# Values of an attention layer stored whole and parted inside each head, with weight sums, constant rows and late loads placed anew, in an fp32 encoder trunk on Trainium2

## The chip, the cores and the metric

The kernel runs on one core of one Trainium2 chip. The metric is the device time of one execution in microseconds (us). A core has five engines that run side by side: PE (TensorE, matmul; PEld is its weight load), DVE (VectorE), ACT (ScalarE), POOL (GpSimd) and SP (SyncE), which here does nothing but issue DMAs. Each engine takes its instructions in order and waits on semaphores for the others; a DMA is issued from an engine's queue, in that queue's order, and lands later.

## The reference

A trunk of two layers over 1024 rows of width 1024, batch 1, all fp32. Layer 0 mixes with a gated MLP (mixer A), layer 1 with chunked attention against a shared K and V; each layer ends with a gated FFN (2816 wide, causal convolution of width 3).

```python
h = x
for l in range(DEPTH):                       # DEPTH = 2
    if l < N_A_LAYERS:                       # l == 0
        h = h + gmlp_mixer(rmsnorm(h, a_norm_g[l]), ...)
    else:                                    # l == 1
        kv = rmsnorm(h, kv_norm_g) @ w_kv
        k_shared, v_shared = jnp.split(kv, 2, axis=-1)   # (B, S, 16, 64) each
        h = h + chunk_attention(rmsnorm(h, b_norm_g[j]), k_shared, v_shared, b_w_q[j], b_rel_bias[j], b_w_o[j])
    h = h + conv_ffn(rmsnorm(h, f_norm_g[l]), f_w_in[l], f_conv_w[l], f_conv_b[l], f_w_down[l])
return rmsnorm(h, final_norm_g)
...
# chunk_attention, for a chunk of 64 queries and its band of 9 chunks of keys
sc = jnp.einsum('bqhd,bkhd->bhqk', qb, kb) + bias
p = jax.nn.softmax(jnp.where(valid, sc, NEG_INF), axis=-1)
o = jnp.einsum('bhqk,bkhd->bqhd', p, vb)
# conv_ffn
a = conv(h @ w_in) + conv_b
up, gate = jnp.split(a, 2, axis=-1)
return (jax.nn.silu(gate) * up) @ w_down
```

## The kernel before

**Products.** Every fp32 operand is parted into a high and a low part (`split`, L138 to L140: ACT casts the high part, `whi` or `yh`; DVE, sometimes POOL, subtracts it, giving `wlo` or `yl`), and a product is three matmuls, high × high, high × low and low × high. The large products are made by seven block products instead of eight (p = 1 to 7; the blocks are A11, A12, ..., and their sums are S1 to S4, made by `block_sum`, L383). A matmul is mostly 128x128 by 128x512.

**Order.** PE's instructions stand as the code is written. A counter, `tick`, adds up the duration of the matmuls issued so far; `put_off(us, fn)` calls `fn` once the counter has moved on by so much, and so places small pieces of work of other engines among the matmuls. Most other engines' instructions, and the DMAs on SP, are put in order by a scheduler that works with an estimated timeline; `issue_after` ties an instruction behind another one.

**Stages, with their places in the profile.** Mixer A to 295 us, FFN of layer 0 to 745. Then `down(0)`, 747 to 957: 77 steps, products 1, 6, 2, 7, 5, 4, 3 with 11 steps each, 12 matmuls a step (L992); each step needs one weight and one operand parted, which `make` does up to three steps ahead from loads of `load`; after the last step of a product `whole` adds the result into the residual h (POOL adds at L960 for products 6 and 7). Beside them the dictionary `aside` calls `value_sums(k)` at steps 46, 53, 60 and 67: load two rows of the value weights (`vr`), multiply both by the norm's gain on POOL (L1047), make four block sums on POOL (L383) and store them to DRAM (`vA`).

`norm` then scales h and parts it (`bc` and `dg` spread the row factors with a small matmul, L210), and makes four operand sums (`sums`). `values` (matmuls at L1141; weights parted into `vwh`, `vwl`) gives V by seven products; `out` parts each of the 8 × 2 result tiles and stores both parts in DRAM (`vd`: vhi and vlo, L1099). Among them q and k of the first pair of heads are made (L181 to L188).

**Heads.** Sixteen heads, 8 steps each, 1068 to 1465 us. A step makes scores (`st`, L1349 and L1351: `qe` by `km`, `qs` by `ks`), has DVE add the bias and ACT make the exponentials `p`, part them (`ph` on ACT, `pl` on POOL, L1363), and two steps later (LAG) multiplies by the value parts `vh`, `vl` (`po`, L1379 to L1383). The row maxima of the next head are made beside it: `mx` (L1196, L1202) and their transposed rows, `mr` (L1211, called by `mx.row`). `qe` and `km` hold some constant rows, copied by `constant_rows` out of tiles `e` (L1158, L1159); parity 0 and 1 of the heads have separate tiles QE, QS, KM, KS, VH, VL. Matmuls of later q and k (`fill`) are spread among the steps; START = 56 pieces of that fill stand before the first head. `stage` loads q and k of a head, `stage_v` its vh and vl. At the end of a pair `den` is inverted through DRAM (`few`, `rden`, `turned`) and the result stored as `osave` in two parts.

**Output projection and FFN of layer 1.** `load_o` loads the parts `oh`, `ol` of half t of the rows; the output projection runs 1465 to 1526 (`wo`), stores h, squares it (`sq`), and the FFN's first weights (`raw<-in_f_win`, cast to `whi`) follow from 1528 us.

## Time and profile before

| | |
|---|---|
| runs | 2181.34, 2181.42, 2186.42 us; median 2181.42 |
| profiled execution | 2186.06 us, of which the span is 2184.3 |
| mean granted TensorE clock | 0.986 |
| DVE, ACT, POOL busy | 74%, 49%, 37% of the span |
| HBM | 252 MB read, 118 MB written |

The profile page groups instructions as "line engine operation out<-in". An arrow with a name behind an idle time says what ended it. The clock is the share of full speed that TensorE was granted. PE's busy time counts matmuls as they are issued one behind the other, so a PE at half clock counts as busy. The stretches in the next section but one are cut at the stages above.

The page's 40 slices of 54.6 us show where PE (tenths busy) and its clock are below the rest:

```
PE   9999999999999999999699999899999999999998
PEclk9999999999999999999899999999999999999999
POOL 1084734333325116442355554431223332341020
DMA  7267623544537966934756766844234454578553
```

The dip is the twentieth slice, 1038 to 1092 us, the start of the heads.

### The profile page before, as it was taken

The numbers are of one execution on the slowest core, as the hardware profiler recorded it, in microseconds if no ns is written. First come the engines' busy times: TensorE is split into PE (matmuls) and PEld (weight loads), VectorE is DVE, ScalarE is ACT, GpSimd is POOL, SyncE is SP. The second block draws the span as 40 slices with busy tenths as digits, with TensorE's granted clock in tenths as the row PEclk, the third lists the DMA queues.
The fourth block names the chain that finished last, engine by engine and source line by source line (L and its number), as shares of the span: only waits on it lengthen the run. The fifth ranks groups of instructions, "written<-read, shape, count | busy, mean of one in ns | idle before, by whom it ended". The sixth has DMA issues, their size and how long they took to land.

```text
span 2184.3 us, 28950 instructions
## 1 busy us (share of the span) xinstructions
PE 2127.6 (97%) x9832; PEld 1770.1 (81%) x9832; DVE 1606.0 (74%) x2355; ACT 1076.2 (49%) x1879; POOL 798.5 (37%) x560
## 2 busy tenths in 40 slices
PE   9999999999999999999699999899999999999998
PEld 8888878888888887777588888787888888888887
DVE  5197889888888668886466655664888888885676
ACT  6423555444555543553366656552554455554443
POOL 1084734333325116442355554431223332341020
PEclk9999999999999999999899999999999999999999
DMA  7267623544537966934756766844234454578553
GB/s 251 75 211 258 240 81 102 169 154 158 171 135 252 341 230 206 315 128 145 212 127 165 178 145 157 228 128 144 83 131 154 153 168 143 184 259 319 193 191 136
DMA packets 224268, 394.09 MB, mean 180 GB/s; under 512 B 61148, under 2 KB 79964, under 8 KB 224120
## 3 DMA queue, kind: packets, MB, share of 16 engines
q1 hardware_dynamic: 221096, 386.79, 55.5%
q10 hardware_dynamic: 3024, 5.46, 0.7%
q8 instruction: 77, 1.26, 0.2%
q14 instruction: 71, 0.58, 0.1%
HBM read 251.99 MB, written 118.08 MB: 169 GB/s over the span
## 4 chain that ended last, share of the span: by engine, by line
PE 83%; DVE 9%; DMA 3%; issue 3%; ACT 1%; SPq 1%; POOL 0%; DVEq 0%; POOLq 0%; ACTq 0%
PE up L992 8%; PE gate L992 8%; PE up L370 7%; PE up L368 7%; PE up L373 7%; PE gate L373 5%; PE gate L368 5%; PE gate L370 5%; PE vps L503 4%; PE qkv L181 2%; PE qkv L188 2%; PE qkv L184 2%; DVE wlo L140 2%; PE v L1141 2%; DVE yl L140 2%
## 5 line engine op out<-in xcount | busy, mean ns | idle before, releaser
L140 DVE TENSOR_TENSOR wlo<-raw,whi 128x512 fp32r<-128x512 f32 x378 | 344.4, 917 | 150.3 <-ACT whi L139 149.9
L139 ACT CAST whi<-raw 128x512 fp32r<-128x512 f32 x378 | 233.3, 620 | 283.8 <-PE gate L992 204.6
L368 PE MATMUL up<-yh,whi 128*128 128x512 f32 x688 | 268.9, 391 | 2.7 <-ACT whi L139 2.0
L370 PE MATMUL up<-yh,wlo 128*128 128x512 f32 x688 | 269.0, 391 | 0.3 <-DVE wlo L140 0.3
L840 POOL TENSOR_TENSOR h<-a 128x512 f32<-128x512 f32 x44 | 83.0, 1887 | 405.5 <-DVE a L832 392.9
L1363 POOL TENSOR_TENSOR pl<-p,ph 128x640 fp32r<-128x640 f32 (+4 forms) x128 | 160.0, 1251 | 167.7 <-ACT ph L1362 125.6
L368 PE MATMUL gate<-th,whi 128*128 128x512 f32 x496 | 192.9, 389 | 0.0
L370 PE MATMUL gate<-th,wlo 128*128 128x512 f32 x496 | 192.9, 389 | 0.0
L373 PE MATMUL up<-yl,whi 128*128 128x512 f32 x688 | 184.3, 389 | 0.0
L140 DVE TENSOR_TENSOR yl<-raw,yh 128x512 fp32r<-128x512 f32 x172 | 153.3, 894 | 8.9 <-ACT yh L139 8.9
L368 PEld LDWEIGHTS up<-yh,whi 128*128 128x128 f32 x688 | 129.5, 188 | 31.1 <-ACT whi L139 2.4
L370 PEld LDWEIGHTS up<-yh,wlo 128*128 128x128 f32 x688 | 129.7, 188 | 27.5 <-DVE wlo L140 0.6
L373 PEld LDWEIGHTS up<-yl,whi 128*128 128x128 f32 x688 | 129.4, 188 | 27.4 <-POOL yl L140 0.5
L373 PE MATMUL gate<-tl,whi 128*128 128x512 f32 x496 | 132.8, 389 | 0.3 <-DVE tl L140 0.3
L139 ACT CAST whi<-S 128x512 fp32r<-128x512 f32 x160 | 99.1, 620 | 66.2 <-PE up L373 60.3
L140 DVE TENSOR_TENSOR wlo<-S,whi 128x512 fp32r<-128x512 f32 x160 | 130.2, 815 | 0.0
L992 PE MATMUL up<-yl,whi 128*128 128x512 f32 (+1 forms) x312 | 122.2, 392 | 4.7 <-DVE yl L140 4.6
L992 PE MATMUL up<-yh,whi 128*128 128x512 f32 (+1 forms) x312 | 121.0, 388 | 2.3 <-ACT yh L139 2.3
L992 PE MATMUL up<-yh,wlo 128*128 128x512 f32 (+1 forms) x312 | 121.1, 388 | 1.7 <-DVE wlo L140 1.7
L992 PE MATMUL gate<-yh,wlo 128*128 128x512 f32 (+1 forms) x312 | 120.7, 387 | 0.0
L992 PE MATMUL gate<-yh,whi 128*128 128x512 f32 (+1 forms) x312 | 120.5, 386 | 0.0
L992 PE MATMUL gate<-yl,whi 128*128 128x512 f32 (+1 forms) x312 | 120.4, 386 | 0.0
(399 smaller groups left out, 5428.9 us busy)
## 6 DMA issues: line engine op xcount, KB each, us to landing
raw<-in_f_win SPq DMA_DIRECT2D x88, 512.0 KB
gT<-h SPq DMA_DIRECT2D x88, 256.0 KB
h<-in_f_wdown SPq DMA_DIRECT2D x44, 512.0 KB
dS<-h SPq DMA_DIRECT2D x88, 256.0 KB
raw<-dS SPq DMA_DIRECT2D x40, 512.0 KB
raw<-gT SPq DMA_DIRECT2D x40, 512.0 KB
gB<-a SPq DMA_DIRECT2D x66, 256.0 KB
raw<-in_f_wdown SPq DMA_DIRECT2D x30, 512.0 KB
```

The costliest lines, as they stand in the source:

```text
L139: behind[S] = S.copy(hi, src)
L140: return eng.tensor_tensor(lo, src, f32(hi), op=ALU.subtract)
L181: nc.tensor.matmul(ps, wh[:, k, :], xs[k][0], start=k == first, stop=False)
L184: nc.tensor.matmul(ps, wl[:, k, :], xs[k][0], start=False, stop=False)
L188: nc.tensor.matmul(ps, wh[:, k, :], xs[k][1], start=False, stop=k == last)
L368: nc.tensor.matmul(ps, wh[:, k, :], xs[k][0], start=first and k == 0, stop=False, skip_group_check=True)
L370: nc.tensor.matmul(ps, wl[:, k, :], xs[k][0], start=False, stop=False, skip_group_check=True)
L373: nc.tensor.matmul(ps, wh[:, k, :], xs[k][1], start=False, stop=k == 3, skip_group_check=True)
L503: nc.tensor.matmul(ps, a, b, start=k == i == 0, stop=k == KD - 1 and i == 2)
L840: G.tensor_tensor(B[n], x, B.get(y) if isinstance(y, str) else y, op=ALU.subtract)
L992: nc.tensor.matmul(ps[:, cs], w[:, ms], x[:, cs], start=q == i == 0 and p in (1, 6, 5, 4), stop=q == NP - 1 and i == 2, skip_group_check=True)
L1363: marks[2] = G.tensor_tensor(pl[:, :n], pf[:, :n], f32(ph[:, :n]), op=ALU.subtract)
```

## The change

- **Value weight sums.** `value_sums(k)` becomes `value_load`, `value_gain` and `value_sum(k, n)`, called at separate steps of `down(0)`. The gain is an ACT multiplication instead of a POOL one; the sums are called one by one every second step.
- **Values.** `out` no longer parts a tile: it copies (ACT) or adds (DVE) into one tile and makes one store to one tensor `vd`. `stage_v` loads a head's values once, into the vl tile; later an ACT copy makes vh and POOL subtracts it from vl in place.
- **Constant rows** of parity 1 are loaded first, into four tiles instead of two in turn; then the `km` and `qe` rows of head 1, bias, the values, and the `qs` and `ks` rows. START is 64.
- **Late loads.** Three parts of half t = 1 are loaded four steps before the last head ends, into QS, VH and VL of the finished parity 0; the remaining five pairs have buffers of their own (six before, besides two in QS and KS). The FFN's first two weight blocks are tied behind the last o load, and its ring of four raw tiles is made of two pools.
- Smaller: the sums in `norm` come 4.5 us apart instead of 2.2; `turned` of the pairs whose result is stored is called after 10.5 instead of 9.0; `mx.row` after 1.2 instead of 0.5.

```diff
-START = 56
+START = 64
...
-                    put_off(7.5 + 2.2 * k, lambda k=k: sums(k))
+                    put_off(7.5 + 4.5 * k, lambda k=k: sums(k))
...
-            open_raw(4)
+            open_raw(3)
+            raws["q"], raws["n"] = raws["ctx"].enter_context(tc.tile_pool(name="wq", bufs=1, reuse_waits="tile")), 0
...
-                behind["load"] = nc.sync.dma_start(raw[i], f_win[l, i * NF + j])
+                with tc.issue_after(behind["o"].ins) if l and j < 2 else ExitStack():
+                    behind["load"] = nc.sync.dma_start(raw[i], f_win[l, i * NF + j])
...
-            with tc.issue_after(behind["adds"].ins):
-                G.tensor_tensor(rows[j], rows[j], cc[:, c:c + 1].broadcast_to([P, T]), op=ALU.mult)
...
+    def value_gain(k):
+        rows = held[k]
+        for j in range(2):
+            S.mul(rows[j], rows[j], col(C_KVG + k + 4 * j))
...
+    def value_sum(k, n):
+        nc.sync.dma_start(va[n][k], block_sum(held[k], n, lambda: vs.tile([P, H], F32, tag="vS", name="vS", bufs=8), G))
+
+    aside = {}
+    for k, (load, first) in enumerate(((24, 28), (28, 36), (38, 48), (48, 57))):
+        aside.setdefault(load, []).append(lambda k=k: value_load(k))
+        aside.setdefault(first - 1, []).append(lambda k=k: value_gain(k))
+        for i in range(4):
+            aside.setdefault(first + 2 * i, []).append(lambda k=k, i=i: value_sum(k, f"S{i + 1}"))
...
-        def out(n, t, m, src, eng=V):
-            hi, lo = (npl.tile([P, H], F32R, tag="acc", name=a, bufs=4) for a in ("vh", "vl"))
-            split(hi, lo, src, eng)
-            for d, a in zip(vd, (hi, lo)):
-                nc.sync.dma_start(d[4 * t + m, :, halves[n]], f32(a))
+        def out(n, t, m, ps, b=None):
+            c = npl.tile([P, H], F32, tag="acc", name="c", bufs=4)
+            if b is None:
+                S.copy(c, ps)
+            else:
+                V.tensor_tensor(c, ps, b, op=ALU.add)
+            nc.sync.dma_start(vd[4 * t + m, :, halves[n]], c)
...
-        def stage_v(hd):
-            for dst, a in zip((VH, VL), vd):
-                nc.sync.dma_start(f32(dst[hd % 2][:, :, rows[hd % 2][0]]),
-                                  a[:, :, hd * 64:(hd + 1) * 64].rearrange("b p c -> p b c"))
+        def stage_v(hd, wait):
+            vh, vl = (v[hd % 2][:, :, rows[hd % 2][0]] for v in (VH, VL))
+            nc.sync.dma_start(f32(vl), vd[:, :, hd * 64:(hd + 1) * 64].rearrange("b p c -> p b c"))
+            put_off(wait, lambda: split(vh, vl, f32(vl), G))
...
-        put_off(7.0, lambda: constant_rows(1, lambda: b2.tile([P, H], F32, tag="o", name="e")))
...
-                waits = (8.0, 8.0) if stays else (9.0, 9.0 if p < LAST - 1 else 6.5)
+                waits = (8.0, 8.0) if stays else (10.5, 9.0 if p < LAST - 1 else 6.5)
...
+        tags = cycle(("o", "o", "den", "den"))
+        constant_rows(1, lambda: b2.tile([P, H], F32, tag=next(tags), name="e"))
         for hs in halves:
-            stage(1, hs)
-        stage_v(0)
+            stage(1, hs, "me")
         bs, bm = {0: new_bias(0, 0)}, {1: new_bias(1, 1)}
+        stage_v(0, 8.0)
+        for hs in halves:
+            stage(1, hs, "s")
...
+            if s == NH * NB - 4:
+                for k, a in enumerate((QS[0], VH[0].rearrange("p n c -> p (n c)"), VL[0].rearrange("p n c -> p (n c)"))):
+                    load_o(k, 1, at=[a[:, hs] for hs in halves])
...
-                stage_v(hd + 1)
+                stage_v(hd + 1, 6.0)
...
-                    put_off(0.5, mx.row)
+                    put_off(1.2, mx.row)
...
-        for k in range(KD):
-            load_o(k, 1, wop, [(QS, KS)[k][0][:, hs] for hs in halves] if k < 2 else None)
+        for k in range(3, KD):
+            load_o(k, 1, wop)
```

Three places of the instruction order carry terms of the prediction. The first is POOL inside `down(0)`. Before, behind the h adds of product 7 (L960, on buffers h_85 and h_86) come the gains (L1047) and the sums (L383):

```order
L960 TENSOR_TENSOR h_86<-h_86,u 128x512
L1047 TENSOR_TENSOR vr<-vr,cc 128x1024 x4
L383 TENSOR_TENSOR vS<-vr 128x512
L383 TENSOR_TENSOR vS<-vS,vr 128x512
```

After (the same lines are L963 and L384), the h adds of product 6 are those on h_84, those of product 7 on h_85 and h_86:

```order
L384 TENSOR_TENSOR vS<-vr 128x512
L384 TENSOR_TENSOR vS<-vr,vS 128x512
L963 TENSOR_TENSOR h_84<-h_84,u 128x512 x4
L384 TENSOR_TENSOR vS<-vr 128x512
L384 TENSOR_TENSOR vS<-vS,vr 128x512
L384 TENSOR_TENSOR vS<-vr 128x512
L384 TENSOR_TENSOR vS<-vr,vS 128x512
L239 TENSOR_TENSOR acc<-acc,sq 128x512
L963 TENSOR_TENSOR h_85<-h_85,u 128x512
```

The gains are gone from POOL; twelve sums (the last two of them shown) stand ahead of product 6's adds, four between them and product 7's.

The second is SP at the start of the heads. Before, behind the last value stores (L1099) come the twelve q and k rows of head 1 (L1182), the values (L1314), bias, and e in two pairs (L1158):

```order
L1099 DMA vlo<-vl 128x512
L1182 DMA km_9468<-k0hi 64x512
L1182 DMA qe_9466<-q0hi 64x512
...
L1182 DMA ks_9469<-k0hi 64x512
L1314 DMA vh_9470<-vhi 128x8x64
L1314 DMA vl_9472<-vlo 128x8x64
L1218 DMA bias<-in_bias 128x256 x2
L1158 DMA e<-in_consts 64x512 x2
...
L156 DMA raw<-in_w_kv 128x1024
L1158 DMA e<-in_consts 64x512 x2
```

After (value store L1117, values L1326, e L1171, rows L1195, bias L1231):

```order
L157 DMA raw<-in_w_kv 128x1024
L1117 DMA vd<-c 128x512
L1326 DMA vl_9399<-vd 128x8x64
...
L157 DMA raw<-in_w_q 128x1024
L1171 DMA e<-in_consts 64x512 x4
L1195 DMA km_9395<-k0hi 64x512
L1195 DMA qe_9393<-q0hi 64x512
...
L1231 DMA bias<-in_bias 128x256 x2
L1195 DMA qs_9394<-q0hi 64x512
```

All four e stand in one piece ahead of the rows of head 1, and the load of the first head's values stands ahead of them.

The third is SP at the end of the heads and the start of layer 1's FFN. Before, the last osave stores (L1449, L1450) stand ahead of every o load of half 1 that has a buffer of its own (L1285, L1286), and the stores of h (L1587) ahead of the weights (L792):

```order
L1449 DMA osave<-oh 128x512
L1450 DMA osave<-ol 128x512
L1580 DMA h_14389<-hsave_89 128x512 x3
L1285 DMA oh<-osave 128x512
...
L1587 DMA hsave_90<-h_14390 128x512 x3
L1587 DMA hsave_90<-h_14389 128x512 x4
L1587 DMA hsave_90<-h_14391 128x512 x3
L792 DMA raw<-in_f_win 128x1024 x2
```

After (o loads L1298 and L1299, osave L1461, h stores L1606, weights L795):

```order
L1298 DMA vh_9397<-osave 128x512
L1228 DMA qe_9393<-mr 1x8x128
...
L1299 DMA vl_9399<-osave 128x512
L1299 DMA vh_9397<-osave 128x512
L1461 DMA osave<-oh 128x512
...
L1606 DMA hsave_90<-h_14339 128x512 x3
L795 DMA raw<-in_f_win 128x1024 x3
L1606 DMA hsave_90<-h_14338 128x512 x4
L1606 DMA hsave_90<-h_14340 128x512 x3
```

Loads into vh and vl (and qs) now stand ahead of the last osave stores, and three of the first four weight loads ahead of seven of the h stores.

More of the change, by code (lines that the diff above doesn't have):

```diff
@@ L97, in new_raw @@
     def new_raw(shape, name="raw"):
-        return raws["p"].tile(shape, F32, tag="raw", name=name)
+        raws["n"] = raws.get("n", 0) + 1
+        return raws["q" if "q" in raws and raws["n"] % 4 == 0 else "p"].tile(shape, F32, tag="raw", name=name)
     def open_places():
@@ L959, in whole @@
                     for x in ((h12,) if p == 6 else (h21, h22)):
-                        behind["adds"] = G.tensor_tensor(x, x, u, op=ALU.add)
+                        G.tensor_tensor(x, x, u, op=ALU.add)
                     return
@@ L980, in down @@
                 if n in aside:
-                    aside[n]()
+                    for fn in aside[n]:
+                        fn()
                 b = "a" if p in (1, 2, 5, 3) else "b"
@@ L1032, in trunk @@
     open_n(0)
-    vd = [dp.tile([NB, P, D], F32, name=f"v{n}") for n in ("hi", "lo")]
+    vd = dp.tile([NB, P, D], F32, name="vd")
     va = {f"S{i}": dp.tile([4, P, H], F32, name=f"vA{i}") for i in range(1, 5)}
@@ L1039, in value_rows, with value_load @@
         return w_kv[KD + n:KD + n + width, :, k, :].rearrange("m p c -> p m c")
-    def value_sums(k):
-        rows = [vs.tile([P, T], F32, tag="vr", name="vr") for _ in range(2)]
+    held = {}
+    def value_load(k):
+        held[k] = [vs.tile([P, T], F32, tag="vr", name="vr") for _ in range(2)]
         for j in range(2):
-            nc.sync.dma_start(rows[j].rearrange("p (m c) -> p m c", c=P), value_rows(0, k + 4 * j))
-            c = C_KVG + k + 4 * j
-            with tc.issue_after(behind["adds"].ins):
-                G.tensor_tensor(rows[j], rows[j], cc[:, c:c + 1].broadcast_to([P, T]), op=ALU.mult)
-        A = {f"A{n + 1}{j + 1}": rows[j][:, halves[n]] for n in range(2) for j in range(2)}
-        for n in va:
-            nc.sync.dma_start(va[n][k], block_sum(A, n, lambda: vs.tile([P, H], F32, tag="vS", name="vS", bufs=8), G))
+            nc.sync.dma_start(held[k][j].rearrange("p (m c) -> p m c", c=P), value_rows(0, k + 4 * j))
+    def value_gain(k):
+        rows = held[k]
+        for j in range(2):
+            S.mul(rows[j], rows[j], col(C_KVG + k + 4 * j))
+        held[k] = {f"A{n + 1}{j + 1}": rows[j][:, halves[n]] for n in range(2) for j in range(2)}
+    def value_sum(k, n):
[6 more added lines that the diff above has]
+            aside.setdefault(first + 2 * i, []).append(lambda k=k, i=i: value_sum(k, f"S{i + 1}"))
     with tc.tile_pool(name="vs", bufs=4, side="right", reuse_waits="tile") as vs:
-        down(0, gs, ds, hsave[0], lambda t, acc: norm(h, acc, t, X), {46 + 7 * k: lambda k=k: value_sums(k) for k in range(4)})
+        down(0, gs, ds, hsave[0], lambda t, acc: norm(h, acc, t, X), aside)
     close_psum()
@@ L1093, in tee @@
                 split(*b, h_all[TEES[RIGHT[p]]][:, :, m * P:(m + 1) * P], G if m % 2 else V)
-        def out(n, t, m, src, eng=V):
-            hi, lo = (npl.tile([P, H], F32R, tag="acc", name=a, bufs=4) for a in ("vh", "vl"))
-            split(hi, lo, src, eng)
-            for d, a in zip(vd, (hi, lo)):
-                nc.sync.dma_start(d[4 * t + m, :, halves[n]], f32(a))
-        def added(ps, b):
-            c = npl.tile([P, H], F32, tag="f", name="c")
-            V.tensor_tensor(c, ps, b, op=ALU.add)
-            return c
+        def out(n, t, m, ps, b=None):
[5 more added lines that the diff above has]
+            nc.sync.dma_start(vd[4 * t + m, :, halves[n]], c)
         def whole(p, m, ps):
@@ L1117, in whole @@
             elif p == 5:
-                out(1, 1, m, added(ps, s1[m]), G)
-                out(0, 1, m, added(ps, x[m]))
+                out(1, 1, m, ps, s1[m])
+                out(0, 1, m, ps, x[m])
             else:
-                out(1, 0, m, added(ps, s1[m]))
+                out(1, 0, m, ps, s1[m])
         todo = [(p, k) for p in order for k in range(4)]
@@ L1149, in trunk @@
     b0 = b0_ctx.enter_context(tc.tile_pool(name="b0", bufs=1, reuse_waits="tile"))
-    QE, QS, KM, KS = ([b0.tile([P, T], F32R, name=f"{n}0")] for n in ("qe", "qs", "km", "ks"))
+    KS, QE, QS, KM = ([b0.tile([P, T], F32R, name=f"{n}0")] for n in ("ks", "qe", "qs", "km"))
     mr0 = b0.tile([NB, P], F32R, name="mr0")
@@ L1282, in load_o @@
     def load_o(k, t, pool=None, at=None):
-        os_[t][k] = oh, ol = at or (tuple(pool.tile([P, H], F32R, tag=n, name=n, bufs=KD - 2) for n in ("oh", "ol")) if pool
+        os_[t][k] = oh, ol = at or (tuple(pool.tile([P, H], F32R, tag=n, name=n, bufs=KD - 3) for n in ("oh", "ol")) if pool
                                     else new_y())
@@ L1294, in trunk @@
             place.append(b1.tile([P, T], F32R, name=f"{n}1"))
-        VH, VL = ([b1.tile([P, NB, P], F32R, name=f"{n}{c}") for c in range(2)] for n in ("vh", "vl"))
-        put_off(7.0, lambda: constant_rows(1, lambda: b2.tile([P, H], F32, tag="o", name="e")))
+        VH, VL = ([(b1 if c else bt).tile([P, NB, P], F32R, name=f"{n}{c}", bufs=1) for c in range(2)] for n in ("vh", "vl"))
         for c in range(2):
```

## The prediction

> **What bounds the kernel now.** I read the page's first section, then busy time by stretches, then the list of PE's waits, then the order in time around the longest. Columns of the stretches: length; busy time (instructions) of PE, PEld, DVE, ACT, POOL; granted clock; DMA share; GB/s.
>
> ```profile
> PE 2127.6 (97%) x9832; PEld 1770.1 (81%) x9832; DVE 1606.0 (74%) x2355; ACT 1076.2 (49%) x1879; POOL 798.5 (37%) x560
> ...
> 747.00:850.00 103.00, 103.00 (x456) 85.26 (x456) 64.48 (x87) 47.07 (x84) 19.65 (x13) 1.00 0.71 247
> 850.00:960.00 110.00, 99.17 (x414) 76.85 (x413) 93.94 (x104) 54.75 (x100) 61.80 (x37) 0.96 0.71 233
> 960.00:1055.00 95.00, 91.18 (x393) 74.03 (x392) 74.67 (x115) 37.84 (x65) 33.54 (x22) 0.97 0.50 166
> ...
> 1070.00:1085.20 15.20, 0.09 (x2) 0.09 (x1) 0.43 (x1) 2.95 (x6) 3.88 (x6) 0.66 0.91 214
> 1085.20:1375.00 289.80, 285.32 (x1539) 249.50 (x1540) 181.46 (x499) 176.22 (x371) 152.07 (x133) 0.99 0.65 153
> 1250.00:1262.00 12.00, 10.03 (x48) 8.63 (x47) 5.58 (x19) 4.08 (x8) 7.31 (x6) 0.86 0.68 173
> 1375.00:1400.00 25.00, 19.12 (x81) 15.68 (x81) 13.27 (x33) 13.31 (x29) 7.33 (x7) 0.80 0.93 244
> 1465.00:1495.00 30.00, 27.27 (x100) 20.30 (x99) 13.12 (x23) 6.75 (x12) 2.59 (x3) 0.83 0.80 271
> 1495.00:1550.00 55.00, 52.66 (x227) 42.63 (x226) 30.19 (x46) 19.05 (x35) 12.85 (x10) 0.97 0.27 92
> ...
> 1980.00:2090.00 110.00, 110.00 (x487) 91.07 (x486) 67.26 (x92) 50.97 (x90) 18.66 (x13) 1.00 0.67 237
> ```
>
> PE is the bound: 97% of the span, and the change takes no matmul away. All that can be won is PE's idle time and the slower clock behind it. A stretch's loss is therefore its length less PE's busy time, plus (1 − clock) × length, good to half a hundredth of the clock. In the down projection of layer 1 (1980 to 2090) PE loses nothing and starts a matmul every 110/487 = 0.226 us; losses of several us each lie between 850 and 1550, where the change works. The waits behind them (total, times, longest):
>
> ```profile
> PE mx L1196 <- issue: 15.1, 1, 15.1
> PE up L992 <- DVE yl L140: 4.6, 9, 1.0
> PE mr L1211 <- ACT p L1359: 3.9, 1, 3.9
> PE wo L181 <- DMA oh<-osave: 2.7, 6, 0.6
> ...
> PE v L1141 <- DVE vwl L140: 2.4, 1, 2.4
> ...
> PE bc L210 <- ACT dg L209: 2.1, 1, 2.1
> PE up L368 <- ACT whi L139: 2.0, 1, 2.0
> ```
>
> What the clock term is, the order in time shows just after the 3.9 us wait: matmuls of 512 columns start 0.43 us apart, not 0.226.
>
> ```profile
> 1381.72 0.63 PE L184 MATMUL qkv<-yh,wlo 128*128 128x512 f32 x1
> 1382.15 0.63 PE L181 MATMUL qkv<-yh,whi 128*128 128x512 f32 x1
> ```
>
> **The change part by part.**
>
> *Value weight sums (850 to 960).* The loss is 10.8 idle + 0.04 × 110 = 4.4, so 15.2 us. POOL's h adds and gains in order of time say why, and groups by line: POOL's sums, an ACT cast (whole span), and one DVE line in 850 to 900 (13 of them) and, as the last row, in 2000 to 2100 (37), inside the second down projection, where no value sums run. After the bar stand the sum in us and the mean of one in ns.
>
> ```profile
> 837.16 13.22 POOL L960 TENSOR_TENSOR h<-h,u 128x512 f32<-128x512 f32 x8 [26.51 <-DVE u L958]
> 850.35 9.24 POOL L1047 TENSOR_TENSOR vr<-vr,cc 128x1024 f32<-128x1024 f32 x4
> ...
> L383 POOL TENSOR_TENSOR vS<-vr 128x512 f32<-128x512 f32 x8 | 13.3, 1660 | 0.1
> ...
> L139 ACT CAST whi<-raw 128x512 fp32r<-128x512 f32 x378 | 233.3, 620 | 283.8 <-PE gate L992 204.6
> ...
> L140 DVE TENSOR_TENSOR yl<-raw,yh 128x512 fp32r<-128x512 f32 x13 | 22.7, 1745 | 0.0
> ...
> L140 DVE TENSOR_TENSOR yl<-raw,yh 128x512 fp32r<-128x512 f32 x37 | 31.9, 862 | 1.0 <-ACT yh L139 1.0
> ```
>
> POOL runs h adds, gains and sums one behind the other. Each step of down has 12 matmuls (12 × 0.226 = 2.71 us) and needs two DVE splits; beside a busy POOL these take 2 × 1.75 = 3.49 us and don't fit, elsewhere 2 × 0.86 = 1.72 and do. The change takes 8 gains of 9.24/4 = 2.31 us, 18.5 us, off POOL and puts them on ACT, which has half of these 110 us free (54.75 busy); my estimate there is two casts of 128x512 (0.62 each) per gain, 10 us in all. The order shows 12 of the 16 sums (1.66 us each, 20 us) in one piece, ahead of product 6's h adds, and the last 4 ahead of product 7's. Such a piece can be borne: POOL was busy from 837.16 and PE still full at 850 (103.00 of 103), since operands are made up to three steps ahead and DVE spares 2.71 − 1.72 = 1 us a step elsewhere. The h adds alone are what the second down projection has, and it loses nothing. I take 13 of 15.2; bounds 0 (the sums collide where they now are) and 15.
>
> The Trainium skill (SBUF — State Buffer, "Who interferes with whom") states that a VectorE instruction with two SBUF inputs contends with a GpSimd instruction that reads SBUF, and that the loser blocks for the whole instruction. The 1.75 us against 0.86 agree. By it the moved sums block too: if all 16 ran without a break, 26.6 us, some ten steps would overrun by 3.49 − 2.71 = 0.78 us each, and this term would be 5 us, not 13; that is within the first rival.
>
> *Norm, values, first q/k (960 to 1055).* The loss is 3.8 + 0.03 × 95 = 2.9, so 6.7 us; the waits on dg (2.1) and vwl (2.4) belong to it: DVE is behind with the value weights' splits. The change splits the first of them among down's steps, spaces the sums of norm at 4.5 instead of 2.2, drops 16 subtractions that parted the outputs (DVE or POOL) and halves 32 stores. I take 4; bounds 0 and 6.5.
>
> *Constant rows (1055 to 1085).* SP's, ACT's and PE's rows:
>
> ```profile
> 1062.12 0.32 SPq L1099 DMA_DIRECT2D vlo<-vl  x1
> 1062.54 1.89 SPq L1182 DMA_DIRECT2D km<-k0hi  x1
> ...
> 1078.91 1.11 SPq L1158 DMA_DIRECT2D e<-in_consts  x2
> ...
> 1084.43 1.14 ACT L1159 CAST km<-e 64x512 fp32r<-64x512 f32 x2 [4.97 <-DMA e<-in_consts]
> ```
>
> SP is in order: the value stores drag to 1062, then 12 rows of k and q, then, among other loads, e in two pairs, since e had two buffers; the second pair, issued at 1078.91, lands 5.5 us later and its casts release mx near 1085. Now the four e go ahead of those rows, into four buffers, behind 16 stores fewer. Issued near 1062.5, with the same 5.5 us and 1.1 us of casts they are done near 1069. PE has run out of work at 1070 (0.09 us busy from there); the fill before the first head is now 8 matmuls longer (8 × 0.226 = 1.8 us) and ends near 1072. So the 15.1 us mostly go; what is late next is the last q and k rows and the vl of the first head, and I leave 1 us for them. I take 14; bounds 8 (the copy of the first vl holds SP for some 6 us) and 17 (with 0.01 × 290 = 2.9 of clock in the next stretch, most of it not of this wait).
>
> *Each head.* One load of 256 KB instead of two; added are one ACT copy vh (512 values a lane, bounded by 0.62) and one POOL subtraction. Nearest rows:
>
> ```profile
> L1363 POOL TENSOR_TENSOR pl<-p,ph 128x512 fp32r<-128x512 f32 x12 | 16.0, 1330 | 21.0 <-ACT ph L1362 21.0
> ...
> 1252.17 1.90 POOL L159 TENSOR_TENSOR raw<-raw,cc 128x1024 f32<-128x1024 f32 x1 [5.05 <-PE st L1349]
> ```
>
> In 1085 to 1375 POOL is busy 52%, ACT 61%, PE 98%; 12 heads × 1.33 = 16 us more make POOL 58%. No throughput limit is near. The danger is order: POOL and ACT stand in line, and if the load is late the p work behind it waits. Such an event is there already: POOL's gain at 1252 sat in front of pl, PE waited 2.0, and the stretch 1250 to 1262 lost 2.0 + 0.14 × 12 = 3.7 us. The subtraction is called 6.0 us after the load's issue, e took 5.5 to land. Later mx.row (0.5 to 1.2) gives the row more time. I take 0; bounds −8 (two such events) and +4 (none is left).
>
> *1375 to 1400.* Loss 5.9 + 0.20 × 25 = 5.0, so 10.9.
>
> ```profile
> 1373.82 0.44 SPq L1457 DMA_DIRECT2D few<-den  x1
> ...
> 1378.47 0.20 DVE L1431 RECIPROCAL few<-few 128x8 f32<-128x8 f32 x1 [2.69 <-DMA few<-den]
> ```
>
> few landed 4.7 us after its issue, behind o loads, and the reciprocal stopped DVE for 2.69, then mr. The reciprocal is now called 1.5 us later and mx.row 0.7 later. 1.5 of 2.7 covers half: I take 5; bounds 0 and 9.
>
> *The last o-parts (1465 to 1495).* Loss 2.7 + 0.17 × 30 = 5.1, so 7.8.
>
> ```profile
> 1464.55 0.32 SPq L1449 DMA_DIRECT2D osave<-oh  x1
> ...
> 1474.23 0.32 SPq L1286 DMA_DIRECT2D ol<-osave  x1
> ...
> 1475.56 0.32 SPq L1286 DMA_DIRECT2D ol<-osave  x1
> ```
>
> SP waits until 1464.55 for the last heads' oh, then issues six pairs of o loads until 1475.56, the last 1.3 us behind the one before; PE waits for six of them. Three parts are now loaded ahead of the blocked store, so five pairs stand behind it: the last is 1.3 us earlier and the first ones no longer matter. I take 2; bounds 0 and 6.
>
> *Start of layer 1 (1495 to 1550).* Loss 2.3 + 0.03 × 55 = 1.7, so 4.0.
>
> ```profile
> 1521.80 4.67 SPq L792 DMA_DIRECT2D raw<-in_f_win  x2
> ...
> 1527.47 1.12 ACT L139 CAST whi<-raw 128x512 fp32r<-128x512 f32 x2
> ```
>
> The weights' casts stood behind sq of the last block. The loads now go behind the last o load, ahead of the stores. I take 3.5; bounds 0 and 4.
>
> Sum: 13 + 4 + 14 + 0 + 5 + 2 + 3.5 = 41.5. The profiled execution took 2186.06 (span 2184.3); that gives 2144.6. The median of the three runs is 2181.42, the others 2181.34 and 2186.42, so the profile is of the slower kind by 4.6; from the median it is 2139.9. I predict 2140.
>
> The Trainium skill (TensorE: Matmul & The Clock Gate, "What's actually happening") states that the array falls to half clock after an idle window of about 3.4 us. The clock of 0.83 in 1465 to 1495, where no wait is over 0.6, does not fit that rule alone. By it the clock parts of the last two terms would not hang on these waits, and the sum would be about 2 us smaller.
>
> **The rivals.**
>
> *The sums still collide.* The vr rows and the vA stores now share SP with down's loads earlier. If a store waits on POOL in front of a load, 850 to 960's loss only moves: 13 back, 2153. For: POOL still has 26.6 us of sums. Against: they stand in pieces of 20 and 7 us, not of 60.
>
> *The constant rows stay late.* Ahead of e on SP stand a raw load and the vl of head 0, which waits for POOL's memset, which waits for a gain whose load is late. If SP is held there some 10 us, 10 of the 14 stay: 2150. That is also how this part would fail to do what it says. For: POOL stood 6.58 us for that load (row below). Against: its gain ended at 1059.5, ahead of the 1062.5 reckoned with.
>
> ```profile
> 1057.62 1.90 POOL L159 TENSOR_TENSOR raw<-raw,cc 128x1024 f32<-128x1024 f32 x1 [6.58 <-DMA raw<-in_w_kv]
> ```
>
> *Slower: the copy waits in every head.* vh<-vl stands on ACT between the exponentials of p. If the load lands after the copy's turn, PE waits as at 1252, 3.7 us with the clock. Fifteen heads are 56 us: 2196. It decides from 41.5/3.7 = 11 heads on; with ten or eleven the time stands still, near 2180. For: 6.0 against 5.5 is a thin margin, and DMA share is 0.65. Against: half as much is loaded, and value matmuls stand two blocks behind the scores.
>
> **How the numbers follow.** Forecast 0.54; sums collide 0.18; rows late 0.14; heads stalling in ten or eleven 0.07, in all 0.07. A change of 0.3%, 6.5 us, is about what a measurement of this kernel can tell from none. The first three are faster by more: 0.86. Ten or eleven heads is the same: 0.07; all is slower: 0.07. The upper bounds of the terms lie 20 us above the values taken; two thirds of that, 14 us, gives the lower end, 2126. The upper end, 2168, is both rivals of the first kind at once, 13 + 10, and 5 for the small terms; the heads' cases, 0.14, lie outside.
>
> **What would show it.** Right: PE full from 850 to 940; mx's wait under 3 us, and km casts before 1072 on the old scale; DVE's reciprocal waiting under 1; no wait on whi at the start of layer 1. Wrong: up L992 still waiting on yl; the e loads behind a long gap of SP; PE waiting for po or mr in most heads with ACT idle in front of vh. If the stretches from 850 to 1550 gain less than 25 us in all, the forecast is wrong whatever the time.

## The result and the profile after

| | before | changed |
|---|---|---|
| median of four runs, us | 2182.20 (2181.34 to 2186.42) | 2153.56 (2148.97 to 2155.22) |
| ratio, 95% interval | | 0.9862 [0.9841, 0.9883] |
| profiled execution, us (span) | 2186.06 (2184.3) | 2148.97 (2147.2) |
| granted TensorE clock | 0.986 | 0.996 |

The change makes the kernel 28.6 us (1.4%) faster; 41.5 was forecast. The two profiles are 37.1 us apart, because that of before is near its slowest run and that of the changed kernel is its fastest. The difference between 28.6 and 37.1 is therefore not to be explained by an edit.

PE's order of matmuls is the same up to the last one of V, so up to there a stage can be cut at the same matmul in both traces. The next two fences show busy time by stretches, first the changed kernel, then the kernel before, with the columns of the prediction. The cuts are: first matmul of the second product of `down(0)`; first of V; last of V; start of head 1; of head 13; of head 15; first `wo` on `oh`; first matmul of layer 1's FFN. (The first product of `down(0)` takes 717 to 747 us in the kernel before and its last matmul is at 943; the 747 to 957 given for the whole of it above is not right. The cut at `wo` lies 0.45 us later in the changed kernel than at the same matmul, since its third part is in `vl` and not in `oh`.)

```profile
747.35:933.72 186.37, 183.58 (x804) 150.98 (x803) 135.96 (x175) 99.05 (x171) 57.91 (x37) 0.99 0.76 261
933.72:1042.50 108.78, 103.06 (x457) 83.65 (x456) 75.43 (x120) 43.29 (x76) 32.66 (x22) 1.00 0.47 151
1042.50:1079.00 36.50, 36.33 (x182) 30.77 (x181) 15.63 (x41) 19.89 (x39) 21.77 (x21) 1.00 0.63 154
1079.00:1355.60 276.60, 270.21 (x1464) 233.31 (x1462) 179.18 (x476) 175.70 (x370) 160.45 (x140) 1.00 0.60 154
1355.60:1404.50 48.90, 42.20 (x219) 35.49 (x219) 36.51 (x87) 31.05 (x65) 24.45 (x20) 0.97 0.71 192
1404.50:1445.80 41.30, 40.01 (x197) 33.92 (x198) 25.65 (x43) 18.94 (x36) 11.52 (x9) 1.00 0.36 118
1445.80:1492.80 47.00, 44.64 (x197) 35.87 (x196) 24.39 (x37) 12.32 (x22) 7.68 (x6) 1.00 0.53 191
```

```profile
747.04:943.10 196.06, 187.33 (x803) 150.40 (x802) 149.08 (x175) 90.59 (x163) 77.16 (x45) 0.98 0.72 245
943.10:1055.00 111.90, 105.98 (x458) 85.74 (x457) 84.01 (x130) 49.03 (x86) 37.82 (x26) 0.97 0.50 167
1055.00:1106.60 51.60, 36.49 (x175) 30.78 (x174) 18.93 (x44) 20.59 (x39) 19.42 (x19) 0.87 0.60 157
1106.60:1388.60 282.00, 273.66 (x1470) 238.69 (x1469) 174.56 (x476) 169.23 (x357) 145.51 (x129) 0.98 0.70 165
1388.60:1434.00 45.40, 41.85 (x219) 35.54 (x218) 34.81 (x88) 30.52 (x63) 21.34 (x19) 0.96 0.78 212
1434.00:1473.60 39.60, 39.43 (x196) 33.41 (x194) 24.17 (x43) 18.55 (x36) 12.17 (x10) 1.00 0.31 104
1473.60:1528.10 54.50, 49.95 (x198) 39.08 (x198) 22.84 (x36) 11.50 (x21) 8.15 (x6) 0.91 0.42 145
```

Row by row the changed kernel is shorter by 9.7, 3.1, 15.1, 5.4, −3.5, −1.7 and 7.5 us. The first three and the last are what the change aims at. In the heads (rows four and five) 327.4 became 325.5; the fill that now stands ahead of the first head, 8 matmuls or 1.8 us, is as much as that, so nothing was won there. PE's list of waits in the changed kernel names what stands there now:

```profile
PE st L1361 <- DMA qe<-mr: 7.2, 6, 3.2
PE wo L182 <- DMA oh<-osave: 2.3, 3, 1.1
PE mr L1224 <- DVE h L1219: 2.0, 1, 2.0
PE v L1154 <- DVE vwl L141: 2.0, 3, 0.7
PE po L1391 <- DVE o L1420: 1.9, 2, 1.3
...
PE up L996 <- DVE wlo L141: 1.6, 1, 1.6
...
PE up L996 <- DVE yl L141: 1.2, 1, 1.2
```

The wait of 15.1 us for `mx` is gone, and so are those on `whi` at the FFN's start and of `mr` for 3.9. The largest is now `st` waiting for the row of maxima (`qe<-mr`), 7.2 us in six waits after 0.7 in two; the two waits of `up` stand near 787 us, where there were none.

### The profile page after: what moved, and what is told of

Its sections match the earlier page's. It is cut to its first block, busy times and chain, and to the rows that moved or that the text cites. A ratio compares the mean times of both kernels' runs of the same rounds, so it can differ in the third digit from the quotient of the medians.

```text
span 2147.2 us, 28888 instructions
## 1 busy us (share of the span) xinstructions
PE 2110.6 (98%) x9832; PEld 1758.6 (82%) x9832; DVE 1586.6 (74%) x2343; ACT 1085.2 (51%) x1891; POOL 795.3 (37%) x564
## 4 chain that ended last, share of the span: by engine, by line
PE 80%; DVE 9%; DMA 5%; issue 2%; ACT 2%; POOL 1%; SPq 0%; DVEq 0%; POOLq 0%; ACTq 0%
PE up L996 8%; PE gate L996 8%; PE up L369 7%; PE up L371 7%; PE up L374 7%; PE gate L369 5%; PE gate L374 5%; PE gate L371 5%; PE vps L504 4%; PE qkv L182 2%; PE v L1154 2%; PE qkv L185 2%; DVE wlo L141 2%; PE qkv L189 2%; PE ups L182 1%
## 5 line engine op out<-in xcount | busy, mean ns | idle before, releaser
L369 PE MATMUL gate<-th,whi 128*128 128x512 f32 x496 | 192.9, 389 | 0.0
L371 PE MATMUL gate<-th,wlo 128*128 128x512 f32 x496 | 192.9, 389 | 0.0
L141 DVE TENSOR_TENSOR yl<-raw,yh 128x512 fp32r<-128x512 f32 x172 | 146.8, 856 | 10.0 <-ACT yh L140 9.2
L140 ACT CAST yh<-raw 128x512 fp32r<-128x512 f32 x190 | 115.1, 617 | 11.4 <-DMA raw<-gB 6.4
```

The costliest lines, as they stand in the source:

```text
L140: behind[S] = S.copy(hi, src)
L141: return eng.tensor_tensor(lo, src, f32(hi), op=ALU.subtract)
L369: nc.tensor.matmul(ps, wh[:, k, :], xs[k][0], start=first and k == 0, stop=False, skip_group_check=True)
L371: nc.tensor.matmul(ps, wl[:, k, :], xs[k][0], start=False, stop=False, skip_group_check=True)
```

## The experiments

All twelve were timed in five rounds. The changed kernel's median, 2153.6, is the measure for those that start from it. They ran in three groups (e1 to e4, e5 to e8, e9 to e12), each on another chip; the kernel before, timed beside each group, took 2181.9, 2181.7 and 2181.0, so medians of different groups compare to about 1 us. Medians with their ranges, and two stages of each profile between the cuts named above (changed kernel: 186.4 and 325.5 us):

| run | what is different | median us (range) | `down(0)` to V | head 1 to head 15 |
|---|---|---|---|---|
| e1 | mx.row after 0.5 | 2153.8 (2147.5 to 2155.5) | 187.5 | 328.9 |
| e2 | constant rows late, in two tiles | 2162.1 (2153.2 to 2170.2) | 184.9 | 324.8 |
| e3 | value sums as before | 2164.3 (2159.3 to 2175.5) | 198.2 | 327.6 |
| e4 | values parted before they are stored | 2159.3 (2155.9 to 2168.7) | 185.8 | 331.4 |
| e5 | reciprocal after 9.0 | 2144.5 (2141.4 to 2146.1) | 187.2 | 320.4 |
| e6 | reciprocal after 13.5 | 2179.0 (2171.1 to 2183.0) | 185.5 | 346.3 |
| e7 | sums behind product 6's adds | 2154.6 (2148.8 to 2156.3) | 186.9 | 328.8 |
| e8 | o-parts loaded as before | 2154.2 (2152.2 to 2156.9) | 185.0 | 330.0 |
| e9 | reciprocal 9.0 and mx.row 0.5 | 2143.3 (2139.5 to 2147.6) | 185.3 | 324.5 |
| e10 | reciprocal 9.0, sums in three pieces | 2150.9 (2143.4 to 2154.0) | 192.9 | 321.1 |
| e11 | kernel before, reciprocal 10.5 | 2180.5 (2173.1 to 2190.9) | 195.6 | 324.9 |
| e12 | weight loads not tied | 2153.0 (2149.5 to 2158.9) | 187.4 | 329.9 |

### e1: the row of maxima as early as before

```diff
-                    put_off(1.2, mx.row)
+                    put_off(0.5, mx.row)
```

> The changed kernel with mx.row called 0.5 us after step 5 again, not 1.2. Theory A (the row of maxima, moved back 0.7 us, now lands in qe after the next head's first score wants it): PE's waits of st on qe<-mr fall from 7.2 us in six to under 2, the time to about 2148 (2145 to 2151). Rival B (mr was waiting for its operands, so the wait only changes its place): mr waits 3 to 6 us in total for DVE or ACT, time 2152 to 2156.

The time did not move, 2153.8. `st` on `qe<-mr` waited 8.6 us, no less than the 7.2 of the changed kernel, and `mr` waited 4.4 us for DVE's maxima, as rival B said. Theory A falls: the moment at which the row is called is not what makes it late. The trace of the changed kernel says what does. SP's queue, in order of time, ahead of head 7:

```profile
1210.37 0.37 SPq L1445 DMA_DIRECT2D rden<-few  x1
1211.57 0.24 SPq L1417 DMA_DIRECT2D den<-den  x1
1212.83 1.41 SPq L1447 DMA_DIRECT2D den<-rden  x2
1214.35 0.69 SPq L1228 DMA_DIRECT2D qe<-mr  x1
```

and PE's rows there:

```profile
1210.33 0.27 PE L1224 MATMUL mr<-ident,mb 128*8 128x128 f32 x1
1216.63 0.35 PE L1361 MATMUL st<-qe,km 128*128 128x256 f32 x1 [1.33 <-DMA qe<-mr]
```

The row's matmul is at 1210.33, its store is issued 4.0 us later. In between SP stands at `den<-rden`, which reads what `rden<-few` has stored and waits until that has landed (18.7 us in 13 such waits in the heads, by SP's list). Where nothing delays it, as in heads 8, 10 and 12, the store follows the matmul by 0.63 us, and `st` starts 4.6 to 4.8 us behind it without a wait.

### e2: the constant rows late again

```diff
-        tags = cycle(("o", "o", "den", "den"))
-        constant_rows(1, lambda: b2.tile([P, H], F32, tag=next(tags), name="e"))
+        put_off(7.0, lambda: constant_rows(1, lambda: b2.tile([P, H], F32, tag="o", name="e")))
         for hs in halves:
-            stage(1, hs, "me")
-        bs, bm = {0: new_bias(0, 0)}, {1: new_bias(1, 1)}
+            stage(1, hs)
         stage_v(0, 8.0)
-        for hs in halves:
-            stage(1, hs, "s")
+        bs, bm = {0: new_bias(0, 0)}, {1: new_bias(1, 1)}
```

> The changed kernel with the constant rows of parity 1 loaded behind the rows of head 1 again, in two tiles by turns. Theory A (their place in SP's order was the whole stall): one wait of mx near 1070 us of 12 to 15 us, time 2166 to 2170. Rival B (half as many value stores free SP early enough by themselves): a wait of 4 to 8 us, time 2157 to 2162.

8.5 us slower in the median, at the far edge of rival B's range. The profile caught the fastest of the seven runs, with this wait:

```profile
PE mx L1209 <- issue: 4.4, 1, 4.4
```

From the end of V to head 1 that run took 43.5 us, against 36.5. The place in SP's order was thus about half of the 15.1 us that the stage had gained (7.0 by this profile, 8.5 by the medians), not all of it. The runs spread over 17 us, more than in any other kernel that starts from the changed one; a stall that hangs on when DMAs land would do that, but it was not shown.

### e3: the value sums as before

```diff
-    for k, (load, first) in enumerate(((24, 28), (28, 36), (38, 48), (48, 57))):
...
+            with tc.issue_after(behind["adds"].ins):
+                G.tensor_tensor(rows[j], rows[j], cc[:, c:c + 1].broadcast_to([P, T]), op=ALU.mult)
...
+    ... {46 + 7 * k: [lambda k=k: value_sums(k)] for k in range(4)}
```

> The changed kernel with the value weight sums as before: steps 46, 53, 60 and 67, gains on POOL. Theory A (a busy POOL stretches DVE's splits until operands are late): PE loses 11 to 13 us between 855 and 900 again, none near 787, time 2161 to 2166. Rival B (this stretch depended on what SP carried, which is less now): a loss of 5 or less, time 2152 to 2157.

10.7 us slower, and `down(0)` takes 198.2 instead of 186.4. PE's waits for it:

```profile
PE up L996 <- DVE yl L141: 6.8, 9, 1.7
PE up L996 <- DVE wlo L141: 2.4, 3, 1.3
```

They stand at 861 to 889 and 940 to 943 us, none near 787. Theory A holds. In the rows one by one, a split of DVE takes 0.68 us where POOL rests and 1.77 beside POOL's sums in the changed kernel, and 2.38 beside the gains (2.34 each) in the kernel before.

### e4: the values parted again before they are stored

```diff
+        def out(n, t, m, src, eng=V):
+            hi, lo = (npl.tile([P, H], F32R, tag="acc", name=a, bufs=4) for a in ("vh", "vl"))
+            split(hi, lo, src, eng)
+            for d, a in zip(vd, (hi, lo)):
+                nc.sync.dma_start(d[4 * t + m, :, halves[n]], f32(a))
...
+            for dst, a in zip((VH, VL), vd):
+                nc.sync.dma_start(f32(dst[hd % 2][:, :, rows[hd % 2][0]]),
+                                  a[:, :, hd * 64:(hd + 1) * 64].rearrange("b p c -> p b c"))
```

> The changed kernel with the values parted and both parts stored at values, and both loaded in each head. Theory A (the parting inside the heads costs nothing, the stores it saves are worth 2 to 5 us at the start of the heads): time 2155 to 2159, a wait near 1056 us of 2 to 5. Rival B (ACT's copy and POOL's subtraction delay p in the heads by 3 to 8 us in all): time 2146 to 2151, PE's waits in the heads that much smaller.

5.7 us slower, just above theory A's range; but the wait that it expected at the start of the heads is small (1.35 us at 1061.73), and the stage from V to head 1 takes only 2.0 us longer. V takes 2.8 us longer (111.6 against 108.8), and the heads, with twice the value loads, 5.9; of this last figure little can be put down to the edit, since e8 and e12, which leave the values alone, take 4.5 and 4.4 longer there.

### e5: the reciprocal after 9.0 us again

```diff
-                waits = (8.0, 8.0) if stays else (10.5, 9.0 if p < LAST - 1 else 6.5)
+                waits = (8.0, 8.0) if stays else (9.0, 9.0 if p < LAST - 1 else 6.5)
```

> The changed kernel with the reciprocal of den called after 9.0 us again, not 10.5. Theory A (called later, its chain few, rden, den through DRAM stands on SP in front of qe<-mr and makes st of the next head late): in heads 3, 7, 11 and 13 SP issues qe<-mr within 2.5 us of the row's matmul, not after 3 to 4; waits of st on qe<-mr fall from 7 to under 4 us, time 2148 to 2152. Rival B (the order on SP is the same, so the store stays late): waits of 7 or more, time 2152 to 2157, and DVE waits for few again.

9.1 us faster than the changed kernel: 2144.5, below theory A's range. The ranges of the two don't touch, though the intervals of their ratios to before overlap by a little (0.9834 [0.9817, 0.9850] and 0.9862 [0.9841, 0.9883]). SP ahead of head 7 in this run, where the row's matmul is at 1210.76:

```profile
1208.10 0.36 SPq L1445 DMA_DIRECT2D rden<-few  x1
...
1209.84 1.11 SPq L1447 DMA_DIRECT2D den<-rden  x2
1211.04 0.54 SPq L1462 DMA_DIRECT2D osave<-ol  x1
1212.28 0.24 SPq L1417 DMA_DIRECT2D den<-den  x1
1213.13 0.70 SPq L1228 DMA_DIRECT2D qe<-mr  x1
```

`rden` is stored 2.7 us ahead of the row's matmul and not with it, its landing is over in time, and `qe<-mr` goes out 2.4 us after the matmul instead of 4.0. In heads 3, 7 and 11 this is 1.6, 2.4 and 2.1 us (3.2, 4.0 and 3.2 in the changed kernel), and `st` waits there 0.3 us in all, not 2.0. DVE's own rows show why 1.5 us were enough. Changed kernel, then e5:

```profile
1210.16 0.19 DVE L1443 RECIPROCAL few<-few 128x8 f32<-128x8 f32 x1
```

```profile
1207.88 0.19 DVE L1443 RECIPROCAL few<-few 128x8 f32<-128x8 f32 x1
```

Called 1.5 us later the reciprocal falls back behind six instructions in DVE's order: relative to the row's matmul it stands at −0.2 and at −2.9 us. Head 13 waits longer than before the edit (3.45 us, SP again at `den<-rden`), so the sum of the waits on `qe<-mr`, 5.5 us, is above what theory A expected. The two waits of `po` for DVE's copy into `o`, 1.9 us, are gone as well.

The longest wait of the changed kernel, 3.25 us ahead of head 14, has another cause. There `qe<-mr` is issued 1.6 us behind the matmul in both kernels, but `st` starts 5.7 us after the issue in the changed kernel and 3.6 in e5: the transfer itself is slow. Two o loads (`yh<-osave`, `yl<-osave`) went out from 2.2 us ahead of it and not from 4.1, and the DMA share until `st` was 1.00 and not 0.75; that they slow it is likely, but not shown. The nine profiles with 10.5 take 5.2 to 6.0 us here, the four with 9.0 take 3.0 to 3.8. So the later reciprocal costs in two ways, and the waits ahead of heads 3, 7, 11 and 13, where SP stands at `den<-rden`, are 2.5 of the 7.2 us.

### e6: the reciprocal later still

`waits` begins with 13.5, else as above.

> The changed kernel with the reciprocal of den called after 13.5 us, so that the second den<-rden of a pair stands behind qe<-mr on SP. Theory A: qe<-mr is issued within 2 us in heads 3, 7 and 11, no wait of st on it there; PE's waits on qe<-mr fall from 7 to about 4 (head 14 stays), time 2147 to 2151. Rival B (the late part is the landing, not the issue, or o's two buffers now block): st still waits 6 or more, or po on DVE o waits over 4, time 2153 to 2160.

What each theory said of the waits came true, and the time lies outside both ranges. `qe<-mr` is issued 0.6 us after the matmul in heads 3, 7 and 11, its wait is down to 1.0 us, and the kernel is 25 us slower. PE's list:

```profile
PE po L1391 <- DVE o L1420: 24.8, 6, 7.1
PE po L1391 <- ACT vh L140: 3.1, 1, 3.1
```

`o` has two buffers; the later the division, the later one comes free for the copy out of PSUM, and the next head's `po` stands. Rival B, with a larger price than expected.

### e7 and e10: other places for the sums

e7 ties all 16 sums behind product 6's adds; e10 (on e5) ties them in pieces of 4, 8 and 4, ahead of, between and behind the two groups of adds. The tie of e7, and that of e10:

```diff
+        with tc.issue_after(behind["adds"].ins):
+            tile = block_sum(held[k], n, lambda: vs.tile([P, H], F32, tag="vS", name="vS", bufs=8), G)
+        nc.sync.dma_start(va[n][k], tile)
```

```diff
+        with tc.issue_after(behind["adds7" if k == 3 else "adds6"].ins) if k else ExitStack():
```

> The changed kernel with the value sums tied behind product 6's h adds on POOL (16 in one piece between the adds of products 6 and 7). Theory A (near 787 us the sums on POOL and their vA stores on SP delay product 6's adds and down's loads): no wait near 787; the stretch from the start of down to the first value matmul is 4 to 5 us shorter, time 2147 to 2151. Rival B (16 in one piece, 27 us, outlast DVE's lead): the loss of 4 to 8 us only moves to 800 to 830, time 2152 to 2158.

> The changed kernel with the reciprocal after 9.0 us and the 16 value sums on POOL in three pieces: 4 ahead of product 6's h adds, 8 between the adds of products 6 and 7, 4 behind product 7's. Theory A (a piece of 8 sums, 13 us, is borne by DVE's lead, one of 12 or 16 isn't): the stretch from the start of down to the first value matmul is 185 us or less, against 187.2, time 2140 to 2143. Rival B (the waits come from SP, whose vA stores wait for POOL between down's loads, however the sums are cut): 186 to 189 us, time 2143 to 2148.

e7: no wait near 787, but three of `up` on `yl` (0.85, 0.66 and 1.18 us) at 806, 815 and 820; `down(0)` 186.9, the time unchanged. Rival B, at the lower end. e10 is 6.3 us slower than e5, and outside both expectations: the waits near 787 stay (0.71 and 1.18 us) though no sum runs in the 21 us ahead of product 6's adds, and a new one of 2.91 us appears at 884.3, where ACT had stood 6.05 us for the value weights' loads (`raw<-in_w_kv`), issued 10.5 us later than in e5, with down's casts behind it. The size of a piece is not the cause near 787. In the changed kernel the twelve sums did not even run in one piece: POOL takes four from 752, four from 760 and four from 777 us, each time as soon as ACT has made the gains. What the waits near 787 begin with is ACT and DVE, here in the changed kernel:

```profile
774.41 1.15 ACT L1055 ACTIVATE vr<-vr,cc 128x1024 f32<-128x1024 f32 x1 [1.24 <-DMA vr<-in_w_kv]
775.91 1.15 ACT L1055 ACTIVATE vr<-vr,cc 128x1024 f32<-128x1024 f32 x1 [0.35 <-DMA vr<-in_w_kv]
777.25 0.62 ACT L140 CAST whi<-raw 128x512 fp32r<-128x512 f32 x1 [0.19 <-DMA raw<-in_f_wdown]
777.90 1.07 DVE L141 TENSOR_TENSOR wlo<-raw,whi 128x512 fp32r<-128x512 f32 x1 [3.92 <-ACT whi L140]
```

```profile
784.37 0.69 DVE L961 TENSOR_TENSOR u<-up,s 128x512 f32<-128x512 f32 x1 [1.24 <-POOL h L963]
785.63 0.69 DVE L961 TENSOR_TENSOR u<-gate,s 128x512 f32<-128x512 f32 x1 [0.56 <-POOL h L963]
786.24 1.13 DVE L141 TENSOR_TENSOR wlo<-raw,whi 128x512 fp32r<-128x512 f32 x1
```

The gains wait on ACT for their loads, with down's cast behind them; DVE gets the cast 3.92 us late and then waits 1.80 us with `u` (two buffers) for POOL's adds, with the split that PE needs behind it. The traces separate the two. In e7 DVE waits for the adds nearly as long (1.30 us) and PE waits for nothing near 787; but no `vr` is loaded between 748 and 790, ACT waits for no load from 760 to 792, and DVE's longest wait for a cast in the 10 us ahead of the adds is this:

```profile
774.34 0.69 DVE L141 TENSOR_TENSOR wlo<-raw,whi 128x512 fp32r<-128x512 f32 x1 [1.42 <-ACT whi L140]
```

In e10 it is 5.54 us, in the changed kernel 3.92. So DVE's lead had been spent on late casts, behind gains and loads that the change had moved there. This is read from the traces; no run moved the loads and gains alone.

### e8 and e12: the late loads

e8 puts all eight o-parts of half 1 behind the last osave store again, with VH and VL of parity 0 in their old pool; e12 takes the tie off the weight loads.

```diff
-                with tc.issue_after(behind["o"].ins) if l and j < 2 else ExitStack():
-                    behind["load"] = nc.sync.dma_start(raw[i], f_win[l, i * NF + j])
+                behind["load"] = nc.sync.dma_start(raw[i], f_win[l, i * NF + j])
```

> The changed kernel with the o-parts of half 1 loaded as before: all eight behind the last osave store, VH and VL of parity 0 in their old pool. Theory A (the early three parts shorten the chain by one pair and start it ahead): the stretch from the first wo on oh to the FFN's first matmul is 3 to 5 us longer, waits on oh 6 times again, time 2156 to 2159. Rival B (the part that went was the start of the FFN, by the earlier weight loads): 0 to 2 us longer, time 2153 to 2155.

> The changed kernel without the tie that puts the FFN's first weight loads of layer 1 behind the last o load (its ring of raw tiles stays in two pools). Theory A (the tie is what starts the casts in time): a wait of up on whi near 1493 us of 1.5 to 2.5 us again, the stretch from the first wo on oh to the FFN 3 to 5 us longer, time 2156 to 2159. Rival B (the scheduler puts the loads early by itself): no such wait, time 2151 to 2156.

Neither moves the time (2154.2 and 2153.0), and neither brings the wait on `whi` back. e12's order shows why: without the tie the first three weight loads go even earlier on SP, ahead of the first h store. The stretch from the first `wo` on `oh` to the FFN was 47.1 us in the changed kernel, 52.0 in e8 and 52.1 in e12, but also 51.2 in e5 and 51.6 in e7, which carry both edits: it varies between executions by as much. The clock accounts for it: e5, e7, e8 and e12 each run 10.2 us of this stretch at half clock, which is 5.1 us of work, and the changed kernel none (see the last section). Without it all five lie between 46.1 and 47.1, so neither edit alone is worth anything that can be seen. What took the `whi` wait away is open: it is 2.0 us in both traces of the old order (before, e11) and in none that starts from the changed kernel; of the edits left, the ring in two pools was not tried.

### e9 and e11: both times undone, and the later reciprocal alone

e9 joins the edits of e1 and e5; e11 is the kernel before with 10.5 for 9.0.

> The changed kernel with both times undone: the reciprocal after 9.0 us and mx.row after 0.5. Theory A (with SP free in time, the earlier row gives st 0.9 us more and nothing takes its place): waits of st on qe<-mr under 5 us, time 2140 to 2144. Rival B (mr then waits for DVE's or ACT's operands, as with the row alone): mr waits 3 us or more, time 2144 to 2148.

> The kernel before with one part of the change alone: the reciprocal of den called after 10.5 us instead of 9.0. The prediction's term (DVE's 2.69 us wait for few ends, mr is in time): the wait of mr near 1380 goes, 2175 to 2178. Theory A (the chain through DRAM comes 1.5 us nearer to qe<-mr and delays st): more waits of st on qe<-mr, 3 us or more against 0.7, time 2184 to 2191. Rival B (it only hurts beside the other edits): 2180 to 2184.

e9 is the fastest version, 2143.3 us, ratio to before 0.9829 [0.9811, 0.9848]; changed kernel 0.9862 [0.9841, 0.9883]. It can't be told from e5 (0.9834 [0.9817, 0.9850]). `st` on `qe<-mr` is down to 2.7 us, `mr` on DVE's maxima up to 5.7: the wait changes its place, as rival B said, in a time that theory A allowed.

e11 stands at 2180.5 against 2181.0, no difference: rival B. The wait of `mr` near 1380 didn't go (it is 3.5 us, at 1374), and one wait on `qe<-mr` of 2.6 us came, ahead of head 14 (0.7 in two before):

```profile
PE mr L1211 <- ACT p L1359: 4.8, 2, 3.5
...
PE st L1349 <- DMA qe<-mr: 2.6, 1, 2.6
```

In that order the reciprocal falls back only ahead of heads 7 and 15, and `st`, 5.7 us behind the row ahead of head 7 and not 4.8, bears it. And DVE still stands for `few`, called later or not:

```profile
1371.21 0.20 DVE L1431 RECIPROCAL few<-few 128x8 f32<-128x8 f32 x1 [2.39 <-DMA few<-den]
```

So the later reciprocal alone neither wins the prediction's 5 us nor costs the 9.

## Why the prediction held and where it failed

The direction, the range and the mechanisms of the two large terms held; the forecast promised 13 us more than came. By the terms of its sum:

- **Value weight sums, 13.** Undone, 10.7; the stage, 9.7. Between 850 and 900 nothing is left of the loss, as forecast, but the first rival came in part: 2.8 us of waits near 787 and a clock of 0.89 from 785 to 800 (another 1.7), at the place to which the sums moved. The rival was right that the vr rows share SP with down's loads. It left out the gains, to which, with their loads, the traces of e7 and e10 point: the prediction reckoned ACT's busy time, 10 us in the free half, but not what stands behind a gain whose load is late. Its piece of 20 us of sums never ran as one, so that DVE's lead bears such a piece was not tested.
- **Norm, values, q and k, 4.** The stage gave 3.1.
- **Constant rows, 14.** The stage gave 15.1. Undone singly, the order of the rows gives back 7.0 us in this stage and the whole values 2.0; the rest goes only with both or has another cause, and no run undid both. The e loads went out at 1044.5, 13 us ahead of the first head, and POOL's memset held nothing up; the rival of late rows fell.
- **Each head, 0.** The copy did wait for its load; the view of what touches `vh` from 1085 to 1400 us says so:

```profile
  DMA vl<-vd: 15.0, 11
```

  11 copies waited 15.0 us in all, ACT's time, and PE's list names no `vh`. With the parting undone (e4) the heads are no faster. The slower rival fell: 6.0 us was indeed thin against the landing, but value matmuls stand far enough behind.
- **1375 to 1400, 5: the step that failed.** The prediction took "the reciprocal is now called 1.5 us later" for a gain, since DVE would no longer stand 2.69 us for `few`, and gave mx.row 0.7 us too. DVE's wait did end, but not by this: with the later call alone it is 2.39 us (e11), and in the changed kernel it is nothing with the call at 9.0 too (e5). In the same way `mr` waits 0.8 us ahead of head 13 at both 10.5 and 9.0, and still 3.5 in e11. Which other part ended these waits was not tried. And the prediction followed the reciprocal to DVE and not to SP. Its result goes through two more DMAs, and `qe<-mr` stands behind the second of them on SP, which issues in order; ahead of head 14 the row lands late instead. Undoing 1.5 us is worth 9.1 by the medians (e5). The two profiles show 5.1 between heads 1 and 15 and 1.6 behind them, but as a whole are only 2.8 apart, because that of e5 lost 5.1 us to the clock in the output projection.
- **The last o-parts and the start of layer 1, 2 + 3.5.** The stretch from head 15 to the FFN went from 94.1 to 88.3 us, 5.8; but 90.9 in e5 and 92.9 in e7. Of the 5.8, 5.1 is the half clock that the kernel before has there and this profile has not. Singly undone, neither edit shows.

Taken without the step that failed, the sum is 36.5, and e5, the same kernel without it, is 36.9 us below the median the prediction started from (2181.42 − 2144.52). That they agree so closely is luck. In the profile of e5, `down(0)` gained 8.9 us and not 13, the heads 7.0 where the sum has nothing, and the last two terms 3.2 and not 5.5: the errors cancel.

## What to carry to other kernels

When an instruction is moved, follow its result through every queue to the last reader, and look at what stands behind each of its DMAs there: in SP's queue here, a dependent pair of transfers (store, then load of the same bytes) made everything behind it wait. A delay that frees one engine has two edges, here the row behind the chain on one side and the two buffers on the other (9.0, 10.5 and 13.5 us gave 2144.5, 2153.6 and 2179.0), so try both directions before it is kept. Work moved out of a crowded stretch should be placed by what else is already in the new one: not by an engine's free time alone, but by what will stand behind it there if its load is late.
